# mix_out as two pairs of column blocks, three of its eight block pairs by Strassen's seven products

## The chip, the core and the metric

The kernel runs on one core of a Trainium2 chip. Times are device microseconds of one execution. Three runs of the kernel before took 1453.27 to 1454.04 us, median 1453.58 us. A separate execution was profiled; the rows below are from it.

TensorE (PE) multiplies; its weight loads (PEld) overlap its matmuls. VectorE (DVE) and ScalarE (ACT) compute elementwise, GpSimd (POOL) does little here. SyncE (SP) and ScalarE issue the DMAs.

## The reference

One decoder layer on 256 tokens of width 2048, in float32: two gated mixers side by side, then cross-attention, MLP and the final norm. The part around the change is:

```python
merged = jax.nn.sigmoid(ga) * y_attn + jax.nn.sigmoid(gc) * y_conv
x = x + merged @ w_mix_out                      # (256, 2048) @ (2048, 2048)
hq = heads(rms_norm(x, norm_xattn) @ wq_x, N_XATTN_HEADS)
mk, mv = jnp.split(rms_norm(mem, norm_mem) @ wkv_x, 2, axis=-1)
...
u = jax.nn.relu(rms_norm(x, norm_mlp) @ w_up)
return x + (u * u) @ w_down
```

## The kernel before

Each float32 operand is split into a rounded high part and the rest (`whi` and `wlo` of a weight, two planes of an activation), and a product is three matmuls: high by high, high by low, low by high (`tok_steps`, lines 108 to 110). ScalarE rounds (`split_w`, line 71), VectorE subtracts (line 72). Weights are read once from DRAM, in loads of 512 KB into four `raw` buffers; `whi` and `wlo` have five buffers each of 128 x 1024.

A product with tokens as rows is made in one of two ways.

- `tok_group` takes one block of 512 columns. It walks the 2048-deep axis in 16 steps of 128, for both halves of the tokens (h), with two PSUM banks: 16 x 2 x 3 = 96 matmuls of 512 columns.
- `pair_group` takes two neighbouring column blocks at once. It walks the axis in eight *block pairs* (two 128-deep steps each). A pair and the two token halves and the two column blocks form a 2 x 2 by 2 x 2 block product. A *plain pair* makes it in eight products (24 matmuls). A *seven-pair* makes it by Strassen's method in Winograd's form, in seven (21 matmuls). It needs sums of weight blocks (`weight_sums`, lines 139 to 142), which are then split like weights, one split of a single block (`split_one`, line 132), and sums of the activation blocks (`act_sums`), which are made once. At the end four block sums (lines 209 to 212) recombine the banks. It uses eight PSUM banks: six `acc` and both `aps`.

PSUM has six `acc` banks and two `aps`; the transposes by which `to_features` turns tokens into features (line 262) also use `aps`. Scratch blocks of 128 x 1024 (`blk`) have three buffers.

Before the change three of the four column pairs of the gate products (line 475) and all of w_down run by `pair_group`, in the order of pairs `MIXED`: seven-pairs 0 to 2 alternate with plain pairs 3 to 5, then 6 and 7. mix_out runs by `residual`: four times `tok_group`, after each an add of the residual rows `xtok` (2 MB, loaded when the gates' buffer `tok` is free), a sum of squares, eight transposes, and four scaled splits into `x2g`. After each of the four stands one call of `memory(j)`: two loads on ScalarE's queue (a quarter of the memory tokens by features, and by tokens), four scaled splits into `memT`, two sums of squares. The memory's key product, from `memT`, follows mix_out.

The order of instructions on each engine is made by the scheduler of the tile layer when the program is built; no table in the kernel sets it. Each engine runs its own list in order and waits on semaphores.

The lines that a sentence can't say, of `pair_group`:

```python
for q, a, b in ((1, act(0, 0), b11), (2, act(1, 0), b21), (3, s4, b22), (5, s1, t1), (7, s3, t3),
                (6, s2, t2), (4, act(1, 1), t4)):
    add(q, pair, a, b, True, True)
...
for q, h, j in ((2, 0, 0), (3, 0, 1), (4, 1, 0), (8, 1, 1)):
```

## Time and profile before

| | |
|---|---|
| median of three runs | 1453.58 us |
| profiled execution | 1452.71 us |
| its span, first to last instruction | 1450.9 us |
| PE busy | 1433.7 us |
| DVE busy | 1025.6 us |
| ACT busy | 752.2 us |
| mix_out stage on PE | about 549 to 640 us |

The span is what the profile shows of the execution; 1.8 us lie around it. A busy share is a share of the span. A matmul's duration in the profile overlaps with the next one's, so PE's pace is read from the distance of two starts, and what an engine waited for from the brackets at the end of a row.

### The profile page before, as it was taken

To read this page: it belongs to the slowest core of one execution; us is meant where nothing else is said; L and a number is where in the kernel's file an instruction comes from. 1 tells how busy PE (TensorE), PEld (TensorE's weight loads), DVE (VectorE), ACT (ScalarE), POOL (GpSimd) and SP (SyncE) were. 2 spreads that over 40 slices of the span, in tenths; PEclk is the share of its full clock that TensorE was granted. 3 is DMA by queue.
4 is the path that set the end of the run, shared out by engine and by line. 5 is a ranking of instruction groups with operands and counts; after the bars stand their busy time and mean duration, and the time that the engine had idled before them with its cause. 6 is when DMAs were issued, how large, how long until landed. Compare 5 with 4: busy or idle time off the path is not lost.

```text
span 1450.9 us, 18458 instructions
## 1 busy us (share of the span) xinstructions
PE 1433.7 (99%) x6923; PEld 1200.4 (83%) x6923; DVE 1025.6 (71%) x1346; ACT 752.2 (52%) x999; POOL 14.4 (1%) x20
## 2 busy tenths in 40 slices
PE   8999999999999999999999999999999999999997
PEld 6888888888878888888888888888888888888875
DVE  6645555667679756654477689668896689866897
ACT  7644444445445545564565455445554555444553
POOL 0000000000000000000000000000000000000010
PEclk9999999999999999999999999999999999999999
DMA  9766555565656767755556566665665556655554
GB/s 320 231 192 185 169 176 172 170 193 189 198 169 196 233 221 266 237 186 186 162 174 183 181 194 211 192 196 170 199 217 190 188 161 212 219 192 183 179 176 145
DMA packets 122938, 283.39 MB, mean 195 GB/s; under 512 B 8928, under 2 KB 9696, under 8 KB 122464
## 3 DMA queue, kind: packets, MB, share of 16 engines
q1 hardware_dynamic: 119088, 273.58, 59.7%
q10 hardware_dynamic: 3760, 8.63, 1.8%
q8 instruction: 54, 0.88, 0.3%
q14 instruction: 36, 0.29, 0.1%
HBM read 280.08 MB, written 2.10 MB: 194 GB/s over the span
## 4 chain that ended last, share of the span: by engine, by line
PE 95%; DVE 2%; DMA 1%; ACT 0%; issue 0%; POOL 0%; SPq 0%; POOLq 0%; DVEq 0%; ACTq 0%
PE acc L83 15%; PE acc L108 13%; PE acc L110 13%; PE acc L109 13%; PE acc L84 8%; PE acc L172 6%; PE acc L173 6%; PE acc L171 6%; PE aps L171 4%; PE aps L172 4%; PE aps L173 4%; DMA raw<-in_w_in_dram 1%; PE acc L87 1%; PE aps L262 1%; DVE wlo L72 1%; PE acc L86 1%
## 5 line engine op out<-in xcount | busy, mean ns | idle before, releaser
L72 DVE TENSOR_TENSOR wlo<-raw,whi 128x1024 fp32r<-128x1024 f32 (+1 forms) x483 | 581.0, 1213 | 307.6 <-ACT whi L71 301.9
L71 ACT ACTIVATE whi<-raw 128x1024 fp32r<-128x1024 f32 (+1 forms) x483 | 500.5, 1050 | 401.2 <-PE acc L110 134.2
L83 PE MATMUL acc<-S,whi 128*128 128x512 f32 x960 | 341.6, 398 | 0.0
L108 PE MATMUL acc<-whi,S 128*128 128x512 f32 x816 | 315.5, 389 | 5.0 <-ACT whi L71 5.0
L110 PE MATMUL acc<-whi,S 128*128 128x512 f32 x816 | 317.3, 389 | 0.0
L109 PE MATMUL acc<-wlo,S 128*128 128x512 f32 x816 | 316.7, 388 | 0.0
L84 PE MATMUL acc<-S,wlo 128*128 128x256 f32 x960 | 269.6, 281 | 0.0
L83 PEld LDWEIGHTS acc<-S,whi 128*128 128x128 f32 x960 | 180.2, 188 | 41.1
L84 PEld LDWEIGHTS acc<-S,wlo 128*128 128x128 f32 x960 | 181.3, 189 | 3.1
L108 PEld LDWEIGHTS acc<-whi,S 128*128 128x128 f32 x816 | 153.6, 189 | 35.4 <-ACT whi L71 5.7
L109 PEld LDWEIGHTS acc<-wlo,S 128*128 128x128 f32 x816 | 153.7, 188 | 30.4
L110 PEld LDWEIGHTS acc<-whi,S 128*128 128x128 f32 x816 | 153.6, 188 | 30.2
L71 ACT ACTIVATE whi<-tsum 128x1024 fp32r<-128x1024 f32 x66 | 69.3, 1058 | 92.0 <-DVE tsum L142 41.8
L172 PE MATMUL acc<-wlo,S 128*128 128x512 f32 x255 | 99.6, 391 | 0.0
L173 PE MATMUL acc<-whi,S 128*128 128x512 f32 x255 | 99.1, 389 | 0.0
L172 PE MATMUL aps<-wlo,S 128*128 128x512 f32 (+1 forms) x253 | 98.3, 388 | 0.0
L173 PE MATMUL aps<-whi,S 128*128 128x512 f32 (+1 forms) x253 | 98.1, 388 | 0.0
L171 PE MATMUL aps<-whi,S 128*128 128x512 f32 (+1 forms) x253 | 95.4, 389 | 0.7 <-DVE tok L610 0.7
L171 PE MATMUL acc<-whi,S 128*128 128x512 f32 x255 | 92.5, 389 | 0.0
L72 DVE TENSOR_TENSOR wlo<-tsum,whi 128x1024 fp32r<-128x1024 f32 x66 | 79.1, 1219 | 15.1 <-ACT whi L71 14.2
L172 PEld LDWEIGHTS acc<-wlo,S 128*128 128x128 f32 x255 | 47.9, 188 | 10.9 <-DVE wlo L72 1.0
L171 PEld LDWEIGHTS aps<-whi,S 128*128 128x128 f32 x253 | 47.5, 188 | 11.3 <-DVE tok L610 1.1
(171 smaller groups left out, 1352.2 us busy)
## 6 DMA issues: line engine op xcount, KB each, us to landing
raw<-in_w_in_dram SPq DMA_DIRECT2D x156, 512.0 KB, 4.4
raw<-in_w_up_dram SPq DMA_DIRECT2D x128, 512.0 KB, 3.9
raw<-in_w_down_dram SPq DMA_DIRECT2D x128, 512.0 KB, 4.7
raw<-in_w_mix_out_dram SPq DMA_DIRECT2D x32, 512.0 KB, 5.0
raw<-in_w_attn_out_dram SPq DMA_DIRECT2D x16, 512.0 KB, 4.9
raw<-in_w_conv_out_dram SPq DMA_DIRECT2D x16, 512.0 KB, 4.5
raw<-in_wkv_x_dram SPq DMA_DIRECT2D x16, 512.0 KB, 4.4
raw<-in_wq_x_dram SPq DMA_DIRECT2D x8, 512.0 KB, 4.0
```

Source lines behind the costliest of these rows:

```text
L71: last_split[0] = nc.scalar.activation(hi[:, k:k + step, :], raw[:, k:k + step, :], AF.Copy)
L72: nc.vector.tensor_sub(lo[:, k:k + step, :], raw[:, k:k + step, :], hi[:, k:k + step, :].bitcast(F32))
L83: nc.tensor.matmul(ps, a, xs(k, 2), start=(k == 0), stop=False)
L84: nc.tensor.matmul(ps[:, S:], c, xs(k, 0), start=False, stop=False)
L86: nc.tensor.matmul(ps[:, S:], c, xs(k, 0), start=False, stop=False)
L87: nc.tensor.matmul(ps, a, xs(k, 2), start=(k == 0), stop=True)
L108: nc.tensor.matmul(ps, xh, wh, start=(k == 0), stop=False)
L109: nc.tensor.matmul(ps, xh, wl, start=False, stop=False)
L110: nc.tensor.matmul(ps, xl, wh, start=False, stop=(k == nk - 1))
L171: nc.tensor.matmul(ps, ah, bh, start=first, stop=False)
L172: nc.tensor.matmul(ps, ah, bl, start=False, stop=False)
L173: nc.tensor.matmul(ps, al, bh, start=False, stop=final)
```

## The change

mix_out is no longer four `tok_group`s but two `pair_group`s (group 1 is columns 0 to 1023, group 2 the rest), with a new order `HIGH`: block pairs 5, 6 and 7 by seven products, and 0 to 4 plain. Pairs 5 to 7 are the features 1280 to 2047 of the merged gates. Their activation sums are made into a new buffer `mS`, where the merged features come out of the transposes (`ev_m`): there a copy to a `blk` goes first, then `act_sums`, then the split. The residual add takes two operations per block in place of one. The transposes of a group follow it, eight features blocks in a row in place of four, and two calls of `memory` stand after each group.

```diff
--- before.py
+++ after.py
@@ -153,7 +153,7 @@
         nc.vector.tensor_sub(s4, a12, s2)
         split_act(dst, kk, t)
 
-    def pair_group(w, c0, kr0, nk, xs, xsum, order, evac, fine=False):
+    def pair_group(w, c0, kr0, nk, xs, xsum, order, evac, fine=False, base=0):
 
         bank = {}
         last = {}
@@ -189,7 +189,7 @@
                 b21, b22 = split_w(r[1])
                 t1, t3 = split_w(ta)
                 t2, t4 = split_w(tb)
-                s1, s2, s3, s4 = (tuple(xsum[:, pair, p, i * P:(i + 1) * P] for p in range(2)) for i in range(4))
+                s1, s2, s3, s4 = (tuple(xsum[:, pair - base, p, i * P:(i + 1) * P] for p in range(2)) for i in range(4))
                 for q, a, b in ((1, act(0, 0), b11), (2, act(1, 0), b21), (3, s4, b22), (5, s1, t1), (7, s3, t3),
                                 (6, s2, t2), (4, act(1, 1), t4)):
                     add(q, pair, a, b, True, True)
@@ -222,6 +222,7 @@
             evac(h, j, bank[8][:, lo], u[:, lo], lo)
             evac(h, j, bank[9][:, lo], u[:, hi], hi)
 
+    HIGH = [(5, True), (0, False), (6, True), (1, False), (7, True), (2, False), (3, False), (4, False)]
     WHOLE, HALVES = (slice(0, 512),), (slice(0, 256), slice(256, 512))
     MIXED = [(0, True), (3, False), (1, True), (4, False), (2, True), (5, False), (6, False), (7, False)]
     MIXED2 = [(0, True), (3, False), (1, True), (4, False), (2, True), (5, False), (6, False), (7, False)]
@@ -473,6 +474,8 @@
                     tok_group(w_in, c0 + j * 512, 0, KD, hx, ev_s)
             else:
                 pair_group(w_in, c0, 0, KD, hx, hS, MIXED, ev_g)
+        if jp:
+            mS = big.tile([P, 3, 2, 512], F32R, name="SS")
         for c in range(2):
             o = c * 512
 
@@ -487,12 +490,38 @@
             tok_group(w_conv_out, jp * 1024 + o, 0, 8, parts_of(acT, 8), ev_v)
 
             def ev_m(b, pt, jp=jp, c=c):
-                split_act(mg, 8 * jp + 4 * c + b, pt.rearrange("p (k s) -> p k s", k=2), 2)
+                k = 8 * jp + 4 * c + b
+                z = pt.rearrange("p (k s) -> p k s", k=2)
+                if k >= 10:
+                    z = block()[:, 0, :].rearrange("p (k s) -> p k s", k=2)
+                    nc.scalar.activation(z, pt.rearrange("p (k s) -> p k s", k=2), AF.Copy)
+                    act_sums(mS, k // 2 - 5, z)
+                split_act(mg, k, z, 2)
             to_features(sg[:, 0, :, o:o + 512], 0, 4, ev_m)
 
     xtok = big.tile([P, 2, D], F32, name="tok")
     nc.sync.dma_start(xtok, xv)
 
+
+    def residual_pairs(w, xs, xsum, dst, gi, name, between):
+        sp = const.tile([P, 2, 4], F32, name=name + "sp")
+        for jp in range(2):
+            def ev(h, j, ps, u, jp=jp):
+                c = 2 * jp + j
+                t = xtok[:, h, c * 512:(c + 1) * 512]
+                nc.vector.tensor_add(t, u, t)
+                nc.vector.tensor_add(t, ps, t)
+                sumsq(sp[:, h, c:c + 1], t, 512)
+
+            def ev_f(b, pt, jp=jp):
+                for i in range(2):
+                    k = 8 * jp + b + i
+                    split_scaled(dst, k, pt[:, i * S:(i + 1) * S], g_of(gi, k))
+            pair_group(w, jp * 1024, 0, KD, xs, xsum, HIGH, ev, base=5)
+            to_features(xtok, 8 * jp, 8, ev_f)
+            between(2 * jp)
+            between(2 * jp + 1)
+        return sp
 
     def residual(w, nk, xs, dst, gi, name, between=lambda j: None):
         sp = const.tile([P, 2, 4], F32, name=name + "sp")
@@ -524,7 +553,7 @@
         for h in range(2):
             sumsq(rmsp[:, h, j:j + 1], mt[:, h, :], 512)
 
-    sp2 = residual(w_mix_out, KD, parts_of(mg), x2g, 1, "r2", memory)
+    sp2 = residual_pairs(w_mix_out, parts_of(mg), mS, x2g, 1, "r2", memory)
     rm = rstd(rmsp, "rm")
     r2 = rstd(sp2, "r2")
 
```

How the scheduler's order moves, at three places.

VectorE, between two column blocks of mix_out before: splits of weights (L72), residual adds (L502), scaled splits of transposed features into `S1` (`x2g`) and of memory into `S3` (`memT`).

```order
L72 TENSOR_TENSOR wlo_4594<-raw_4591,whi_4593 128x1024
L72 TENSOR_TENSOR wlo_4600<-raw_4597,whi_4599 128x1024
L502 TENSOR_TENSOR tok_4397<-acc_4403,tok_4397 128x512
L72 TENSOR_TENSOR wlo_4630<-raw_4627,whi_4629 128x1024
L502 TENSOR_TENSOR tok_4397<-acc_4404,tok_4397 128x512
L72 TENSOR_TENSOR wlo_4636<-raw_4633,whi_4635 128x1024
L72 TENSOR_TENSOR wlo_4666<-raw_4663,whi_4665 128x1024
L72 TENSOR_TENSOR wlo_4672<-raw_4669,whi_4671 128x1024
L252 SCALAR_TENSOR_TENSOR S1_4399<-aps_4555,gcol_88,S1_4399 128x256
L252 SCALAR_TENSOR_TENSOR S1_4399<-aps_4564,gcol_88,S1_4399 128x256
L72 TENSOR_TENSOR wlo_4702<-raw_4699,whi_4701 128x1024
L252 SCALAR_TENSOR_TENSOR S3_4400<-blk_5131,gcol_88,S3_4400 128x256 x4
```

VectorE at the boundary of group 1 and group 2 after the change: `blk_4820` and `blk_4836` are the memory blocks of `memory(0)` and `memory(1)`, L513 the adds that empty group 1's banks, `tsum` the weight sums of group 2's seven-pairs.

```order
L253 SCALAR_TENSOR_TENSOR S3_4428<-blk_4820,gcol_88,S3_4428 128x256 x4
L142 TENSOR_TENSOR tsum_4857<-raw_4854,tsum_4857 128x512
L72 TENSOR_TENSOR wlo_4871<-tsum_4856,whi_4870 128x1024
L253 SCALAR_TENSOR_TENSOR S3_4428<-blk_4836,gcol_88,S3_4428 128x256 x4
L513 TENSOR_TENSOR tok_4425<-acc_4461,tok_4425 128x512
L513 TENSOR_TENSOR tok_4425<-acc_4465,tok_4425 128x512
L139 TENSOR_TENSOR tsum_4947<-raw_4943 128x512
L72 TENSOR_TENSOR wlo_4875<-tsum_4857,whi_4874 128x1024
L513 TENSOR_TENSOR tok_4425<-aps_4481,tok_4425 128x512
L513 TENSOR_TENSOR tok_4425<-aps_4515,tok_4425 128x512
L72 TENSOR_TENSOR wlo_4911<-raw_4906,whi_4910 128x1024
L72 TENSOR_TENSOR wlo_4915<-raw_4908,whi_4914 128x1024
```

Two memory blocks' splits now stand ahead of the adds that empty the banks, and weight sums and splits of the next group between them.

ScalarE at the memory loads in mix_out before (`S_4400` is `memT`):

```order
L523 DMA blk<-in_mem_dram 128x2x512
L71 ACTIVATE whi<-raw 128x1024
L519 DMA blk<-in_memf_dram 128x1024
L247 ACTIVATE S_2391<-aps 128x2x256 x2
L251 ACTIVATE S_4400<-blk,gcol 128x256 x4
L71 ACTIVATE whi<-raw 128x1024 x2
L523 DMA blk<-in_mem_dram 128x2x512
L71 ACTIVATE whi<-raw 128x1024 x2
```

ScalarE at the same place after the change (`S_4428` is `memT`, `tsum` a weight sum of group 2):

```order
L548 DMA blk<-in_memf_dram 128x1024
L71 ACTIVATE whi<-raw 128x1024 x2
L252 ACTIVATE S_4428<-blk,gcol 128x256 x4
L552 DMA blk<-in_mem_dram 128x2x512
L548 DMA blk<-in_memf_dram 128x1024
L71 ACTIVATE whi<-tsum 128x1024
L252 ACTIVATE S_4428<-blk,gcol 128x256 x4
L552 DMA blk<-in_mem_dram 128x2x512
L71 ACTIVATE whi<-tsum 128x1024
L71 ACTIVATE whi<-raw 128x1024 x2
```

In the piece of before one load and one block's scaling belong to this boundary; after the change two do, and the first block's scaling stands ahead of the issue of the second block's load.

PE at a boundary of column blocks before: transposes of finished columns stand among the matmuls of the next, which use other banks (`acc`).

```order
L109 MATMUL acc_4589<-wlo_4600,S2_2391 128x512
L262 MATMUL aps_4555<-ident_108,tok_4397 128x128
L262 MATMUL aps_4564<-ident_108,tok_4397 128x128
L110 MATMUL acc_4589<-whi_4599,S2_2391 128x512
...
L110 MATMUL acc_4590<-whi_4599,S2_2391 128x512
L262 MATMUL aps_4555<-ident_108,tok_4397 128x128 x3
L262 MATMUL aps_4564<-ident_108,tok_4397 128x128 x3
L108 MATMUL acc_4590<-whi_4599,S2_2391 128x512
```

PE in group 2 after the change: the last transposes of group 1 (`aps_4802`, `aps_4811`), and, eleven matmuls further, the first matmul of group 2 on an `aps` bank (`aps_4902`).

```order
L171 MATMUL acc_4878<-ohi_5036,S2_2391 128x512
L263 MATMUL aps_4802<-ident_108,tok_4425 128x128 x4
L263 MATMUL aps_4811<-ident_108,tok_4425 128x128 x4
L171 MATMUL acc_4898<-whi_4965,SS_4061 128x512
...
L173 MATMUL acc_4882<-whi_4994,S2_2391 128x512
L172 MATMUL acc_4886<-wlo_4995,S2_2391 128x512
L173 MATMUL acc_4886<-whi_4994,S2_2391 128x512
L171 MATMUL aps_4902<-whi_4874,S2_2391 128x512
L172 MATMUL aps_4902<-wlo_4875,S2_2391 128x512
```

The products on `aps` banks, which stood in program order among the others, now come after the transposes have left these banks.

## Rows read from the trace of the kernel before

**Rows 1.** The page: busy time by engine; the granted clock in 40 slices.

```profile
PE 1433.7 (99%) x6923; PEld 1200.4 (83%) x6923; DVE 1025.6 (71%) x1346; ACT 752.2 (52%) x999; POOL 14.4 (1%) x20
...
PEclk9999999999999999999999999999999999999999
```

**Rows 2.** Waits of PE: line, whom for, us in total, times, longest.

```profile
PE acc L108 <- ACT whi L71: 5.0, 2, 4.6
PE aps L171 <- DVE tok L610: 0.7, 1, 0.7
PE acc L171 <- ACT ohi L131: 0.5, 1, 0.5
PE acc L171 <- ACT whi L71: 0.4, 1, 0.4
PE acc L108 <- ACT SS L247: 0.3, 1, 0.3
PE acc L172 <- DVE olo L132: 0.2, 1, 0.2
```

**Rows 3.** Timeline of PE in mix_out: start, us, engine, line, tiles, count.

```profile
540.06 0.39 PE L110 MATMUL acc<-whi,S 128*128 128x512 f32 x1
...
551.85 0.39 PE L108 MATMUL acc<-whi,S 128*128 128x512 f32 x1
...
557.56 0.82 PE L262 MATMUL aps<-ident,tok 128*128 128x128 f32 x6
558.13 0.48 PE L108 MATMUL acc<-whi,S 128*128 128x512 f32 x1
```

**Rows 4.** Windows (mix_out; two w_down groups): length, busy PE PEld DVE ACT POOL, clock.

```profile
549.00:640.00 91.00, 91.00 (x419) 75.32 (x418) 56.66 (x72) 53.66 (x89) 0.00 (x0) 1.00 0.72 238
1019.00:1060.00 41.00, 41.00 (x181) 33.71 (x180) 38.31 (x46) 20.77 (x23) 0.00 (x0) 1.00 0.58 181
1060.00:1102.00 42.00, 42.00 (x200) 35.12 (x200) 33.34 (x37) 19.07 (x21) 0.00 (x0) 1.00 0.71 232
```

**Rows 5.** Timeline of DVE, in w_down and in mix_out.

```profile
1035.11 1.21 DVE L72 TENSOR_TENSOR wlo<-raw,whi 128x1024 fp32r<-128x1024 f32 x1
1036.25 0.68 DVE L210 TENSOR_TENSOR blk<-acc,blk 128x512 f32<-128x512 f32 x1
1036.85 0.68 DVE L211 TENSOR_TENSOR blk<-acc,blk 128x512 f32<-128x512 f32 x1
...
587.48 4.63 DVE L72 TENSOR_TENSOR wlo<-raw,whi 128x1024 fp32r<-128x1024 f32 x4 [0.40 <-ACT whi L71]
...
552.94 2.85 DVE L252 SCALAR_TENSOR_TENSOR S<-blk,gcol,S 128x256 fp32r<-128x256 f32 x7
```

**Rows 6.** Timeline of ACT in mix_out, with its DMA issues (ACTq).

```profile
555.04 1.06 ACT L71 ACTIVATE whi<-raw 128x1024 fp32r<-128x1024 f32 x1 [0.32 <-PE acc L110]
...
561.75 1.71 ACT L251 ACTIVATE S<-blk,gcol 128x256 fp32r<-128x256 f32 x4 [2.58 <-DMA blk<-in_memf_dram]
563.36 1.05 ACT L71 ACTIVATE whi<-raw 128x1024 fp32r<-128x1024 f32 x1
564.01 0.37 ACTq L523 DMA_DIRECT2D blk<-in_mem_dram  x1
```

**Rows 7.** The memory loads by features: issue min/median/max ns, and landing.

```profile
L519 ACTq DMA_DIRECT2D blk<-in_memf_dram x4: 347/347/347, 501.7 to 578.3; - x4
...
DMA to landing us min/median/max: 5.1/5.8/5.9
```

**Rows 8.** Groups of DVE, shapes apart: count, busy us, mean ns, idle before.

```profile
L72 DVE TENSOR_TENSOR wlo<-raw,whi 128x1024 fp32r<-128x1024 f32 x475 | 575.6, 1222 | 306.8 <-ACT whi L71 301.2
L209 DVE TENSOR_TENSOR blk<-acc,blk 128x512 f32<-128x512 f32 x11 | 7.5, 682 | 0.0
L252 DVE SCALAR_TENSOR_TENSOR S<-blk,gcol,S 128x256 fp32r<-128x256 f32 x16 | 6.7, 479 | 3.9 <-ACT S L251 3.9
```

**Rows 9.** mix_out's loads: landing; issues from 555 to 575 us; SP, ACT.

```profile
DMA to landing us min/median/max: 3.8/5.0/13.4
...
raw<-in_w_mix_out_dram SPq DMA_DIRECT2D x6, 512.0 KB, 8.0
tok<-in_x_dram SPq DMA_DIRECT2D x1, 2048.0 KB, 11.6
...
558.41 0.37 SPq L494 DMA_DIRECT2D tok<-in_x_dram  x1
558.87 40.11 SPq L61 DMA_DIRECT2D raw<-in_w_mix_out_dram  x15
...
572.39 1.06 ACT L71 ACTIVATE whi<-raw 128x1024 fp32r<-128x1024 f32 x1 [6.08 <-DMA raw<-in_w_mix_out_dram]
```

**Rows 10.** Timelines of DVE and PE in the second gate group.

```profile
430.20 0.69 DVE L139 TENSOR_TENSOR tsum<-raw 128x512 f32<-128x512 f32 x1 [3.19 <-DMA raw<-in_w_in_dram]
...
430.89 0.49 PE L171 MATMUL acc<-ohi,S 128*128 128x512 f32 x1 [0.47 <-ACT ohi L131]
```

## The prediction

> **What bounds the kernel now.** I read the page first: TensorE (PE) is busy for 99% of the span at the full granted clock, VectorE (DVE) for 71% [rows 1]. Then the waits of PE: the few rows there are add up to some 7 us, 5.0 of them at the start of the kernel [rows 2]. So the kernel lasts as long as PE's instruction stream. A matmul taken away is worth its own step, and everything else is free until PE waits for it. Third, PE's steps in the mix_out stage: 52 matmuls of 512 columns start between 540.06 and 551.85 us, 0.2267 us each, and six transposes take 558.13 - 557.56 = 0.57 us, 0.095 us each [rows 3]. Last, the load beside PE. In the whole mix_out stage (549 to 640 us) DVE is busy 56.7 of 91 us; where `pair_group` already runs twice in a row, in w_down, it is busy 38.3 of 41 us and then 33.3 of 42 us, and PE still does not wait [rows 4]. So a pair group nearly fills DVE, and mix_out has other DVE work that w_down has not.
>
> **What it removes.** Three of eight block pairs take 21 matmuls in place of 24, in two column pairs: 2 x 3 x 3 = 18 matmuls, 18 x 0.2267 = 4.1 us off PE [rows 3]. The transposes stay at 32, the weight bytes at 32 loads of 512 KB. By the instruction orders nothing moves ahead of the first mix_out weights or behind the attention that follows, so no other stage has a term.
>
> **What it adds, on DVE.** Durations overlap by a little, so I count from start to start: a 512-wide operation 0.60 us (1036.25 to 1036.85), a 1024-wide split 1.14 us (1035.11 to 1036.25, and four in 4.63 us), a 256-wide scaled split 0.40 us (seven in 2.85 us) [rows 5]. A plain pair costs two splits, 2.28 us. A seven-pair costs four sums, one 512-wide split and three 1024-wide ones: 4 x 0.60 + 0.60 + 3 x 1.14 = 6.42 us, 4.14 us more. Six of them: 24.8 us. Four block sums per group: 2 x 4 x 0.60 = 4.8 us. Sixteen residual adds in place of eight: 4.8 us. The activation sums of `mS` are three times four 128-wide operations and a split; I take 1.4 us each from the 0.60 us of the split and an estimate of 0.2 us for a 128-wide one, together 4.3 us. The sum is 38.7 us. With the 56.7 us of before DVE has 95 us of work in a stage in which PE has 91 - 4.1 = 87 us. Buffers can lend a few us of that, so the place at which DVE is furthest behind decides.
>
> **That place is the boundary of the two groups.** In the last third of group 1 DVE is tied to PE: the split of pair 3 (`wlo_4693`) needs one of five `whi` buffers, and the first to come free is that of pair 7, when PE has done its last matmul on `whi_4619`. I set that moment to 0. ScalarE's split follows, 1.06 us [rows 6], with hand-overs 1.2 us by my estimate. From there DVE's order holds, up to the second scaled split of `aps_4802`: 13 splits of 1024 (14.8 us), 26 operations of 512 (15.6 us) and 15 scaled splits of 256 (6.0 us), 36.4 us in all. PE has in the same piece, up to the first matmul on `aps_4902`, 137 matmuls and 16 transposes: 31.1 + 1.5 = 32.6 us. That matmul needs the PSUM bank that held `aps_4802`. So it comes (1.2 + 36.4) - 32.6 = 5.0 us late even if DVE waits for nothing.
>
> **DVE waits there too.** Both `memory` calls now stand at one place. Their blocks come free when the sums `x`, `y` and `z` of group 1 have been used. The last reader of `x` ends at 1.2 + 2 x 1.14 + 3 x 0.60 = 5.3 us. A memory load lands 5.8 us after its issue [rows 7]: 11.1 us. ScalarE then scales four pieces, 1.71 us as at 561.75 us, and only behind them does it issue a DMA, as at 564.01 us [rows 6]. So the second `memory` load is issued at about 13.3 us (0.4 us of it for the load of `mt` between them) and lands at 19.1 us; the first piece is ready at 19.6 us. DVE stands at its first split for that load at 5.3 + 4 x 1.14 + 9 x 0.60 + 4 x 0.40 = 16.9 us and waits 2.7 us. Behind this instruction are queued the four adds that free group 1's banks, the splits of group 2's first two pairs and all eight scaled splits of the transposes; PE waits for each of them in turn. The delay goes through: 5.0 + 2.7 = 7.7 us. From the other sides: with landings of 5.1 and 5.9 us in both loads [rows 7] the wait is 1.3 to 2.9 us; without any, the stall stays at 5.0 us.
>
> Two rules would move this term. The four memory loads of before landed after 5.1 to 5.9 us [rows 7]. The Trainium skill (SBUF — State Buffer, "The DMA setup-cost knee") puts a transfer at about 2 us and its bytes at 436 GB/s. An estimate by that page is 3.2 us for 512 KB; two loads in a row would then be 5.2 us sooner, the wait gone, and the total 2.7 us less. The trace does not agree, so I keep its landings. A DVE operation of 0.68 us is followed by the next after 0.60 us [rows 5]. The Trainium skill (VectorE: DVE Perf Modes, "The DRAIN you can't avoid") says that the next operation does not start before the pipe of the one before is empty. If that meant durations end to end, 1.222, 0.682 and 0.479 us [rows 8], the 36.4 us would be 40.8 and the total 4.4 us more. The starts go against it.
>
> **A smaller term in group 1.** The third seven-pair's second row load is issued just before the 2 MB residual load. DVE has 4.4 us of other work before it needs that row, and PE a margin of 1.9 us beyond; the landing thus costs PE what it exceeds 6.3 us by. Landings in this stage are 3.8 us at the least, 5.0 in the median and 13.4 us at the most, with 8.0 in the median beside the residual load [rows 9]: 0 to 7.1 us, 1.7 at 8.0 us. I take 0.7 us. That such a late row stops PE is seen in the gates: DVE waited 3.19 us for one at 430.20 us, and PE 0.47 us at 430.89 us for what hangs on it [rows 10]. ScalarE gets no term of its own: six more 1024-wide splits at 1.06 us [rows 6] and, at about half of that each, 14 more 512-wide splits and copies are some 14 us on top of 53.7 of 91 us [rows 4]. After the boundary DVE is again tied to PE by buffers, and the next stage's weights need only half as many splits per matmul, so nothing is lost there; the lost time is not regained either, since PE was full.
>
> **Sum.** The profiled execution took 1452.71 us, span 1450.9 and 1.8 us around it. -4.1 + 7.7 + 0.7 = +4.3 us, so 1457.0 us. The median of the runs, 1453.58 us, lies 0.9 us above the profiled execution, so 1457.9 us is what I expect of the runs. Of the term of 7.7 us, a 3% error in the steps moves 1.1 us and the memory landings 1.4 us; with 0 to 1.7 us for group 1 the forecast's own range is 1455 to 1461 us.
>
> **Rivals.**
> 1. *The buffers hold as in the other pair groups.* DVE gets ahead in the plain pairs, the boundary is only rough, and PE waits no more than in all the pair groups of before together, the 1.8 us of the four L171 and L172 rows [rows 2]. For it: DVE at 38.3 of 41 us in w_down did no harm [rows 4], and PE waits for pair groups so little in the whole trace. Against it: the five buffers are what ties DVE, and between the two w_down groups stand no transposes and no memory loads. -4.1 + 0.6 = -3.5 us, 1450.1 us: faster. It decides if fewer than about 1.2 us of DVE's 7.7 us lag reach PE. Chance 0.11.
> 2. *DVE is behind, but not through memory.* The second memory load lands before DVE gets there and part of the 5.0 us is made good by steps that are shorter beside PSUM reads. A stall of 4 to 5 us: -4.1 + 4.5 = +0.4 us, 1454.0 us, no change. For it: a 5.1 us landing already halves the wait. Chance 0.20.
> 3. *The residual load decides.* The row load beside it lands after 13.4 us as one did before [rows 9], PE waits 7.1 us in group 1, of which the tie to PE's buffers afterwards spares nothing: +4.3 + 6.4 = +10.7 us, 1464 us. Against it: that landing was of the load issued at 558.87 us, behind the residual load (ScalarE got it at 572.39 us); this one is issued ahead. Chance 0.12.
> The forecast itself has 0.57.
>
> **Chances and range.** A measurement tells 0.2%, 2.9 us, from no change. Faster by more: nearly all of rival 1 with its small stalls, 0.10. Within: rival 2, and the low end of the forecast, 0.23. Slower: the rest of the forecast and rival 3, 0.67. The range 1451.5 to 1463.5 us leaves out most of rival 1 and half of rival 3, and takes in everything else.
>
> **What would show it.** Right: PE's matmul records in the mix_out stage fall by 18; the waits of PE have new rows that name L171 to L173 and the transposes, waiting for VectorE, within some 25 us around the end of group 1, and sum to 6 to 11 us; the largest single one is the first matmul on an `aps` bank in group 2; DVE is busy all but 3 us there, and has one wait for the memory load of some 2.7 us through ScalarE. Wrong: PE with no gap at the boundary (then the five buffers did not tie DVE, rival 1); a gap there with DVE idle for other reasons, as row loads (rival 3); or new waits outside 545 to 645 us, since the order elsewhere is unchanged.

## The result and the profile after

The changed kernel takes 1466.89 us (median of four runs, 1464.44 to 1468.69) against 1453.42 us for the kernel before beside it: a ratio of 1.0085, 95% interval 1.0068 to 1.0102. It is slower, as predicted, but by 13.5 us where 4.3 were predicted, and above the upper end of the range, 1463.5 us. The profiled execution took 1468.69 us, its span 1466.9 us.

The page of the changed kernel: busy time by engine, and the granted clock in 40 slices.

```profile
PE 1439.1 (98%) x6905; PEld 1201.9 (82%) x6905; DVE 1062.7 (72%) x1413; ACT 764.2 (52%) x1019; POOL 15.5 (1%) x20
...
PEclk9999999999999999899999999999999999999999
```

Against [rows 1], 18 matmul records are gone, as they should be, and yet PE's busy time has *grown* by 5.4 us. That contradiction is the first clue, and the clock line holds the second: one slice shows 8 where all of before showed 9.

The waits of PE after (line, whom for, us in total, times, longest):

```profile
PE acc L108 <- ACT whi L71: 4.8, 1, 4.8
PE acc L171 <- ACT whi L71: 4.2, 2, 3.9
PE acc L171 <- ACT ohi L131: 2.1, 2, 1.5
PE aps L171 <- DVE S L253: 1.9, 1, 1.9
PE acc L171 <- DVE tok L639: 1.3, 2, 0.9
PE aps L263 <- DVE tok L513: 1.3, 1, 1.3
```

The first row is the kernel's start, in [rows 2] as well. To place the rest I lay the two profiles side by side at two points of PE: the last transposes ahead of mix_out and the first matmul of w_up. Before, then after:

```profile
534.38 0.82 PE L262 MATMUL aps<-ident,tok 128*128 128x128 f32 x6
...
740.82 0.39 PE L83 MATMUL acc<-S,whi 128*128 128x512 f32 x1
```

```profile
537.91 0.82 PE L263 MATMUL aps<-ident,tok 128*128 128x128 f32 x6
...
755.35 0.39 PE L83 MATMUL acc<-S,whi 128*128 128x512 f32 x1
```

This stretch, which I call the stage below, took 206.44 us before and 217.44 us after: 11.0 us more. 3.5 us were lost ahead of it and 1.5 us behind it. Inside it, the timeline of PE with every row after 540 us and ahead of 700 us that waited, and some of their neighbours:

```profile
560.98 0.50 PE L171 MATMUL aps<-whi,S 128*128 128x512 f32 x1 [0.36 <-ACT blk L497]
...
598.53 0.39 PE L173 MATMUL acc<-whi,SS 128*128 128x512 f32 x1
602.81 1.22 PE L171 MATMUL acc<-whi,S 128*128 128x512 f32 x2 [3.90 <-ACT whi L71]
603.83 0.63 PE L171 MATMUL acc<-whi,SS 128*128 128x512 f32 x1
604.26 0.63 PE L172 MATMUL acc<-wlo,SS 128*128 128x512 f32 x1
...
608.30 0.48 PE L172 MATMUL acc<-wlo,S 128*128 128x512 f32 x1
...
613.46 0.50 PE L172 MATMUL acc<-wlo,SS 128*128 128x512 f32 x1 [0.31 <-DVE wlo L72]
...
615.24 0.50 PE L171 MATMUL acc<-ohi,S 128*128 128x512 f32 x1 [0.58 <-ACT ohi L131]
...
618.59 0.51 PE L172 MATMUL acc<-wlo,S 128*128 128x512 f32 x1 [0.26 <-DVE wlo L72]
...
619.40 0.40 PE L173 MATMUL acc<-whi,S 128*128 128x512 f32 x1
621.67 0.59 PE L171 MATMUL aps<-whi,S 128*128 128x512 f32 x1 [1.87 <-DVE S L253]
622.06 0.63 PE L172 MATMUL aps<-wlo,S 128*128 128x512 f32 x1
...
625.39 0.39 PE L171 MATMUL aps<-whi,S 128*128 128x512 f32 x1
...
658.80 1.25 PE L263 MATMUL aps<-ident,tok 128*128 128x128 f32 x8 [1.27 <-DVE tok L513]
```

Read the starts as well as the brackets. From 603.83 to 604.26 us one matmul takes 0.43 us; its step is 0.2267 us in [rows 3]. Steps as long stand behind the wait at 621.67 us. The windows of PE show why (length, busy PE PEld DVE ACT POOL, granted clock):

```profile
599.00:603.00 4.00, 0.19 (x1) 0.19 (x2) 3.30 (x7) 3.84 (x7) 0.00 (x0) 0.80 0.52 162
603.00:607.00 4.00, 4.00 (x10) 3.02 (x11) 4.00 (x6) 4.00 (x10) 0.00 (x0) 0.50 0.01 3
617.00:622.00 5.00, 2.87 (x11) 1.66 (x10) 5.00 (x10) 2.25 (x6) 0.00 (x0) 0.99 0.44 120
622.00:626.00 4.00, 4.00 (x12) 3.15 (x11) 1.74 (x2) 1.06 (x1) 0.00 (x0) 0.59 0.31 115
```

After PE stood still, its granted clock was 0.50, the lower of its two levels (1.2 against 2.4 GHz), for some 4 us. A PE at half clock counts as busy, so the page's busy time grows while work was taken away.

Now the stage's account. The gaps, from start to start less one step, are 4.05 us at 602.81, 0.48, 0.75, 0.43 and, at 621.67, 2.04 us: 7.75 us at the boundary. Nine matmuls and eight transposes from 602.81 to 608.30 us took 5.49 us; at the steps of [rows 3] they take 9 x 0.2267 + 8 x 0.095 = 2.80 us. Nine matmuls from 621.67 to 625.39 us took 3.72 us in place of 2.04. So 2.7 + 1.7 = 4.4 us went to the half clock. The wait at 560.98 us cost 0.6 us, that at 658.80 us 1.4 us. -4.1 + 7.75 + 4.4 + 0.6 + 1.4 = 10.1 us; 0.9 of the 11.0 us is spread over smaller shifts that I did not place. This says how PE spent the time, not what each term would give back if it alone were gone.

Who holds PE at 602.81 us is seen on ScalarE (ACTq is its DMA issue):

```profile
585.72 0.35 ACTq L548 DMA_DIRECT2D blk<-in_memf_dram  x1
...
592.65 0.51 ACT L252 ACTIVATE S<-blk,gcol 128x256 fp32r<-128x256 f32 x1 [4.16 <-DMA blk<-in_memf_dram]
...
593.08 0.48 ACTq L548 DMA_DIRECT2D blk<-in_memf_dram  x1
...
599.16 0.51 ACT L252 ACTIVATE S<-blk,gcol 128x256 fp32r<-128x256 f32 x1 [3.85 <-DMA blk<-in_memf_dram]
...
600.77 1.04 ACT L71 ACTIVATE whi<-tsum 128x1024 fp32r<-128x1024 f32 x1
601.72 1.99 ACT L71 ACTIVATE whi<-raw 128x1024 fp32r<-128x1024 f32 x2
```

The second `memory` load is issued only when the first has landed, at 593.08 us, beside the second of the four scalings and not behind all four as predicted. ScalarE then stands for it, and the weight splits for PE's next matmuls are queued behind. VectorE waits beside it, 1.24 us for the first load's scaling and 3.08 us for the second's:

```profile
599.70 1.68 DVE L253 SCALAR_TENSOR_TENSOR S<-blk,gcol,S 128x256 fp32r<-128x256 f32 x4 [3.08 <-ACT S L252]
...
621.04 0.87 DVE L253 SCALAR_TENSOR_TENSOR S<-aps,gcol,S 128x256 fp32r<-128x256 f32 x2
```

The first of the two splits at 621.04 us takes 0.48 us and frees the `aps` bank, and PE starts on it at 621.67 us. Between these two rows VectorE stands for only 0.85 us (0.67 and 0.18 us for `whi`). So this matmul could hardly have come sooner, however soon PE had done what stands ahead of it: the 3.90 us wait for `whi` and the 2.7 us of slow steps behind it lie inside a time that VectorE needed anyway. Two paths hold PE here at once, ScalarE's line and VectorE's.

The loads by features now land after (minimum, median, maximum)

```profile
DMA to landing us min/median/max: 6.0/6.5/9.2
```

where [rows 7] had 5.1, 5.8 and 5.9. The two of the boundary took 6.9 and 6.1 us, the last one, behind group 2, 9.2 us, and VectorE stood for it:

```profile
655.28 0.49 DVE L253 SCALAR_TENSOR_TENSOR S<-blk,gcol,S 128x256 fp32r<-128x256 f32 x1 [5.11 <-ACT S L252]
```

The Trainium skill (SBUF — State Buffer, "The DMA setup-cost knee") would give an estimate of 3.2 us for their 512 KB; the trace does not agree, with 6.0 us at the least.

### The profile page after: what moved, and what is told of

Same layout as the page of the kernel before. It is cut to its first block, busy times and chain, and to the rows that moved or that the text cites. A ratio compares the mean times of both kernels' runs of the same rounds, so it can differ in the third digit from the quotient of the medians.

```text
span 1466.9 us, 18527 instructions
## 1 busy us (share of the span) xinstructions
PE 1439.1 (98%) x6905; PEld 1201.9 (82%) x6905; DVE 1062.7 (72%) x1413; ACT 764.2 (52%) x1019; POOL 15.5 (1%) x20
## 4 chain that ended last, share of the span: by engine, by line
PE 83%; DMA 7%; DVE 7%; ACT 1%; issue 1%; POOL 0%; POOLq 0%; ACTq 0%; DVEq 0%; SPq 0%
PE acc L83 15%; PE acc L108 10%; PE acc L109 10%; PE acc L110 10%; PE acc L84 7%; PE acc L172 5%; PE acc L171 5%; PE acc L173 5%; PE aps L171 4%; PE aps L172 3%; PE aps L173 3%; DMA raw<-in_w_down_dram 3%; DVE wlo L72 3%; DMA blk<-in_memf_dram 2%; DMA raw<-in_w_mix_out_dram 2%
## 5 line engine op out<-in xcount | busy, mean ns | idle before, releaser
L72 DVE TENSOR_TENSOR wlo<-raw,whi 128x1024 fp32r<-128x1024 f32 (+1 forms) x477 | 573.5, 1213 | 275.6 <-ACT whi L71 270.9
L108 PE MATMUL acc<-whi,S 128*128 128x512 f32 (+1 forms) x688 | 265.8, 390 | 4.8 <-ACT whi L71 4.8
L110 PE MATMUL acc<-whi,S 128*128 128x512 f32 (+1 forms) x688 | 267.4, 389 | 0.0
L109 PE MATMUL acc<-wlo,S 128*128 128x512 f32 (+1 forms) x688 | 267.3, 388 | 0.0
L108 PEld LDWEIGHTS acc<-whi,S 128*128 128x128 f32 x688 | 129.9, 189 | 30.8 <-ACT whi L71 5.4
L110 PEld LDWEIGHTS acc<-whi,S 128*128 128x128 f32 x688 | 129.9, 189 | 25.4
L109 PEld LDWEIGHTS acc<-wlo,S 128*128 128x128 f32 x688 | 129.9, 189 | 25.3
L71 ACT ACTIVATE whi<-tsum 128x1024 fp32r<-128x1024 f32 x78 | 81.8, 1058 | 97.4 <-DVE tsum L142 42.3
L172 PE MATMUL acc<-wlo,S 128*128 128x512 f32 (+1 forms) x301 | 117.7, 392 | 0.3 <-DVE wlo L72 0.3
L172 PE MATMUL aps<-wlo,S 128*128 128x512 f32 x299 | 117.5, 393 | 0.0
L171 PE MATMUL aps<-whi,S 128*128 128x512 f32 x299 | 114.5, 394 | 2.9 <-DVE S L253 1.9
L173 PE MATMUL aps<-whi,S 128*128 128x512 f32 x299 | 117.1, 392 | 0.0
L173 PE MATMUL acc<-whi,S 128*128 128x512 f32 (+1 forms) x301 | 116.9, 389 | 0.0
L171 PE MATMUL acc<-whi,S 128*128 128x512 f32 (+1 forms) x301 | 109.5, 392 | 3.9 <-ACT whi L71 3.9
L72 DVE TENSOR_TENSOR wlo<-tsum,whi 128x1024 fp32r<-128x1024 f32 x78 | 93.8, 1223 | 12.3 <-ACT whi L71 11.3
L171 PEld LDWEIGHTS acc<-whi,S 128*128 128x128 f32 x301 | 56.5, 189 | 16.7 <-ACT whi L71 4.6
L171 PEld LDWEIGHTS aps<-whi,S 128*128 128x128 f32 x299 | 56.9, 190 | 16.2 <-issue 2.3
```

The source lines that it names most:

```text
L71: last_split[0] = nc.scalar.activation(hi[:, k:k + step, :], raw[:, k:k + step, :], AF.Copy)
L72: nc.vector.tensor_sub(lo[:, k:k + step, :], raw[:, k:k + step, :], hi[:, k:k + step, :].bitcast(F32))
L108: nc.tensor.matmul(ps, xh, wh, start=(k == 0), stop=False)
L109: nc.tensor.matmul(ps, xh, wl, start=False, stop=False)
L110: nc.tensor.matmul(ps, xl, wh, start=False, stop=(k == nk - 1))
L171: nc.tensor.matmul(ps, ah, bh, start=first, stop=False)
```

## The experiments

Two theories stood first. **A:** ScalarE's queue, held by the second memory load, stops PE, and the halved clock adds to it. **B:** VectorE simply has more work at the boundary than PE's time covers. **C** came after the first four runs: whatever stands on ScalarE and VectorE ahead of the scaled splits that free the two `aps` banks reaches PE, since products 4 and 8 of the next group need these banks. Each ratio is to the kernel before in the same comparison. The stage is from one profile each.

| run | ratio to before, 95% interval | stage, us |
|---|---|---|
| changed kernel | 1.0085 [1.0068, 1.0102] | 217.4 |
| 1 memory constant | 1.0064 [1.0046, 1.0083] | 214.8 |
| 2 loads first | 1.0039 [1.0025, 1.0053] | 212.5 |
| 3 sums late | 1.0031 [1.0014, 1.0048] | 212.8 |
| 4 plain pairs only | 1.0062 [1.0045, 1.0078] | 216.8 |
| 5 transposes later | 1.0053 [1.0034, 1.0073] | 213.8 |
| 6 = 2 and 5 | 1.0024 [1.0012, 1.0035] | 210.0 |
| 7 = 2, 3 and 5 | 0.9995 [0.9983, 1.0007] | 206.5 |
| 8 = 4 with filling | 1.0057 [1.0035, 1.0079] | 215.0 |
| 9 = 2 and 3 | 1.0033 [1.0018, 1.0048] | 210.3 |
| 10 = 7, transposes spread | 0.9976 [0.9967, 0.9985] | 203.7 |
| changed kernel again | 1.0075 [1.0061, 1.0089] | 216.4 |

**1. Memory constant.** The loads by features are left out and a constant tile is scaled in their place, behind the copy of bank 1 in each group, so `memT` holds other values. (In all the edits below `...` marks lines that are not shown; where an edit repeats that of an earlier run, only some of its lines stand here.)

```diff
-        m = block().rearrange("p a (b s) -> p (a b) s", s=S)
-        nc.scalar.dma_start(m, memf[:, 4 * j:4 * j + 4, :])
-        for k in range(4):
-            split_scaled(memT, 4 * j + k, m[:, k, :], g_of(2, 4 * j + k))
+        with tc.issue_after(last_p1[0].ins):
+            for k in range(4):
+                split_scaled(memT, 4 * j + k, ones, g_of(2, 4 * j + k))
```

> Left out: the four loads of the memory tokens by features; the scalings that read them read a constant tile instead, and stand behind the copy of bank 1 in each group. Theory A (ScalarE's queue stands still for the second memory load, PE waits 3.9 us for a weight split behind it, and pays again by the halved clock): the 3.9 us wait of PE at the end of group 1 is gone, ScalarE has no idle time of 4 us there, and the total falls by 5 to 8 us, to 1459 to 1462 us. Theory B (VectorE has too much work at the boundary, whoever waits first): ScalarE's idle time goes, PE's waits stay within 2 us of the changed kernel's, total 1464 to 1468 us.

It took 1464.0 us. The 3.9 us wait for ScalarE is gone, but another came, in the waits of PE:

```profile
PE aps L173 <- DVE S L255: 5.0, 1, 5.0
```

The total is B's, the place is the one that the prediction named, and 5.0 us is what it gave for "DVE waits for nothing". But that agreement is luck, and the run does not decide for B. With no load to wait for, the scheduler put the eight scalings of *group 2's* memory blocks into this stretch, 3.2 us of VectorE's work at the 0.40 us of a step, right ahead of the splits that free the bank:

```profile
612.29 2.46 DVE L255 SCALAR_TENSOR_TENSOR S<-ones,gcol,S 128x256 fp32r<-128x256 f32 x6
```

The eight of group 1, in turn, left the boundary for 574 us. What VectorE does here without a wait for the loads and without these is seen in run 2.

**2. Loads first.** Four `blk` buffers; both loads are issued ahead of both scalings.

```diff
-    blk = ctx.enter_context(tc.tile_pool(name="blk", bufs=3))
+    blk = ctx.enter_context(tc.tile_pool(name="blk", bufs=4))
...
+        for i in range(2):
+            m = block().rearrange("p a (b s) -> p (a b) s", s=S)
+            nc.scalar.dma_start(m, memf[:, 4 * (j + i):4 * (j + i) + 4, :])
+            ms.append(m)
```

> Four scratch blocks in place of three, and both memory loads of a boundary issued ahead of the first scaling; the work is the same. Theory A: one landing is waited for in place of two, the wait of PE for the split behind it shrinks from 3.9 to under 1.5 us, total 4 to 7 us less than the changed kernel, 1460 to 1463 us. Theory B: no more than 2 us less, 1465 to 1468 us.

1460.02 us, the stage 4.9 us shorter: A's outcome, but waits of 0.2 to 1.9 us are left at the boundary (`wlo` 1.01, `ohi` 1.56, an `aps` bank 1.89 us), so not A alone. VectorE does not stand for a memory load at the boundary any more. Even so the gaps of PE up to the first matmul on an `aps` bank (1.17, 0.89, 1.73, 0.41 and 2.05 us, start to start less a step) add up to 6.3 us, where the prediction gave 5.0 us for "DVE waits for nothing". That part of B is shown.

**3. Sums late.** Group 2 begins with two plain pairs.

```diff
+    LATE = [(0, False), (1, False), (5, True), (2, False), (6, True), (3, False), (7, True), (4, False)]
...
-            pair_group(w, jp * 1024, 0, KD, xs, xsum, HIGH, ev, base=5)
+            pair_group(w, jp * 1024, 0, KD, xs, xsum, LATE if jp else HIGH, ev, base=5)
```

> Group 2 takes plain pairs 0 and 1 before its seven-pairs, so that the weight sums of pair 5 leave the boundary (4.1 us less VectorE work there); the memory loads stay. Theory A: the wait of PE for ScalarE behind the memory load stays at 3 to 5 us, total within 2 us of the changed kernel. Theory B: the waits of PE in group 2 fall by about 4 us and with them one stretch of half clock (2 us), total 1460 to 1463 us.

1459.4 us, the stage 4.7 us shorter, a little more than B expected and with the memory loads untouched. The largest wait of PE at the boundary is 1.06 us, where A had expected 3 to 5 us, although VectorE stands 4.90 us for the second load here.

**4. Plain pairs only.** Two groups of eight plain pairs: no weight or activation sums at all, and the 18 matmuls are back.

```diff
-    HIGH = [(5, True), (0, False), (6, True), (1, False), (7, True), (2, False), (3, False), (4, False)]
+    HIGH = [(k, False) for k in range(8)]
```

> Both groups by pair_group with plain pairs alone: no weight sums, activation sums or block sums, 384 matmuls as before; boundary, transposes and memory loads stay where the change puts them. Theory A: the wait behind the memory load stays and costs 3 to 4 us and a stretch of half clock, total 1457 to 1461 us. Theory B: without the sums VectorE keeps up, PE waits under 1 us, total 1453 to 1455 us.

1463.27 us, above what either theory expected. PE has one large wait, and for eight matmuls behind it half the clock:

```profile
612.54 0.77 PE L171 MATMUL aps<-whi,S 128*128 128x512 f32 x1 [6.54 <-DVE S L257]
```

ScalarE shows its origin:

```profile
608.76 1.71 ACT L256 ACTIVATE S<-blk,gcol 128x256 fp32r<-128x256 f32 x4 [4.50 <-DMA blk<-in_memf_dram]
```

VectorE waits 4.52 us beside it, and the scaled splits that free the banks are queued behind on both engines. So the pairing by itself, eight banks in use and two `memory` calls in one place, costs a stall without any of Strassen's sums. This run made theory C.

**5. Transposes later.** All 32 of them follow the memory key product.

```diff
-            to_features(xtok, 8 * jp, 8, ev_f)
+            feats.append(lambda jp=jp, ev_f=ev_f: to_features(xtok, 8 * jp, 8, ev_f))
...
     by_features(wkv_x, xm, rm, mkT)
+    for feat in feats:
+        feat()
```

> All 32 feature transposes of the mixed rows (with their scaled splits) stand behind the memory key product, so that the two aps banks belong to products 4 and 8 alone at the boundary of the column groups; memory's loads and scalings stay where they are. Theory A (ScalarE's queue held by the second memory load): the wait for whi remains with 3 to 4 us, followed by steps of 0.43 us, and only the aps waits go: 1462 to 1466 us. Theory B (VectorE has too much at the boundary): the scaled splits of the transposes are gone from it, so 1456 to 1460 us and no wait above 1.3 us. Theory C (what stands on ScalarE and VectorE ahead of the hand-over of the two aps banks reaches TensorE): the aps waits of 1.9 and 1.3 us and the slow steps behind the first go, the whi wait shrinks only as far as the queue is shorter: 1458 to 1462 us.

1461.3 us. Both `aps` waits are gone; the wait for `whi` stays at 3.67 us, and half-clock steps follow it until 604.5 us. C and A are both seen in one trace: the banks were one way to PE, ScalarE's line the other.

**6. Transposes later and loads first**, the edits of 2 and 5.

```diff
+    blk = ctx.enter_context(tc.tile_pool(name="blk", bufs=4))
...
+            feats.append(lambda jp=jp, ev_f=ev_f: to_features(xtok, 8 * jp, 8, ev_f))
```

> As the run with the transposes behind the memory key product, and both memory loads are issued ahead of the scalings, with four blk buffers in place of three. Theory C with A: neither the banks nor the loads hold anything at the boundary, no wait above 1 us in mix_out, no half-speed steps there, so the 18 matmuls saved show: 1449 to 1453 us, up to 1455 if the gates stall as in the changed kernel. Theory B: waits for wlo and ohi stay (VectorE's sums): 1456 to 1460 us.

1458.89 us. At the boundary only waits of 0.2 to 0.8 us are left and no half clock, but the stage is still 3.6 us longer than before. Higher than C and A expected: waits for `ohi` and `wlo` stay at the boundary, as B said, and behind it come new ones, 0.56, 0.56 and 1.35 us between 660 and 719 us.

**7. All three**, the edits of 2, 3 and 5.

```diff
+            pair_group(w, jp * 1024, 0, KD, xs, xsum, LATE if jp else HIGH, ev, base=5)
...
+            feats.append(lambda jp=jp, ev_f=ev_f: to_features(xtok, 8 * jp, 8, ev_f))
```

> As the run before it, and the second column group begins with two plain block pairs, so that its first sums come some 10 us after the boundary. Theory C with A: nothing left for it to mend, within 1.5 us of the run without it. Theory B: 3 us faster than the run without it or more.

1454.15 us; the stage is 3.6 us shorter than without the late sums, which is B's expectation. With two of the three alone, loads and transposes (run 6) or loads and sums (run 9), the kernel stays slower than before. Whether the loads are needed beside the other two is not shown: the third pair was not run. The stage now equals that of before, 206.45 against 206.44 us. Of the 4.1 us saved, 2.8 us are spent again on four small waits, 0.36, 0.56, 0.56 and 1.35 us, the last three behind the boundary, between 656 and 714 us.

**8. Plain pairs with filling.** As 4, with 28 useless matmuls more (the first of a product, repeated and overwritten) ahead of the place of the 6.54 us.

```diff
+            for _ in range(28 if base and c0 and q == 3 and first else 0):
+                nc.tensor.matmul(ps, ah, bh, start=True, stop=True)
             nc.tensor.matmul(ps, ah, bh, start=first, stop=False)
```

> The kernel of plain pairs alone (384 matmuls), with 28 useless matmuls more (a product's first one, repeated and overwritten) in the second column group, ahead of the place where TensorE stood 6.54 us. If the half granted clock follows the pause, TensorE's granted clock stays at 1.00 through the stretch, no step of 0.43 us stands there, and the time is that of the kernel without them or 1 to 2 us below it (1461 to 1463.5), though 6.3 us of work were added. If the low clock has nothing to do with the pause, the slow steps stay and the time is 0 to 2 us above; if the pause is not a wait with an end of its own, the time grows by 6 us, to 1469.

1462.46 us, though 28 x 0.2267 = 6.3 us of work were added; the ratios, 1.0057 and 1.0062, do not tell the two kernels apart. The stage is 1.8 us *shorter*, in one profile each. Windows of run 4, then of this run:

```profile
604.00:612.00 8.00, 2.01 (x13) 1.51 (x12) 3.33 (x9) 3.27 (x9) 0.00 (x0) 0.82 0.41 159
612.00:616.00 4.00, 3.46 (x8) 2.82 (x9) 0.79 (x2) 0.28 (x1) 0.00 (x0) 0.50 0.00 0
```

```profile
604.00:612.00 8.00, 8.00 (x41) 6.68 (x40) 3.52 (x8) 3.53 (x8) 0.00 (x0) 1.00 0.08 31
612.00:616.00 4.00, 4.00 (x19) 3.31 (x18) 1.42 (x2) 2.51 (x3) 0.00 (x0) 1.00 0.00 0
```

ScalarE still waits 3.77 us for the memory load, so the origin is unchanged; PE only did not stand. With the pause the low clock is gone: nine steps on the `aps` bank took 2.07 us here and 3.77 us in run 4. The half clock follows the pause, and here it is a price of its own. The Trainium skill (TensorE: Matmul & The Clock Gate, "HAM oscillation — how this bites in real kernels") tells of a kernel whose PE waits for a transfer ahead of each piece of work and starts each piece throttled. Run 4 agrees, with a clock of 0.50 behind 6.54 us; that the short wait of 1.87 us in the changed kernel did it too goes beyond the page's case.

**9. Loads first and sums late**, the edits of 2 and 3, transposes left at the boundary.

```diff
+            pair_group(w, jp * 1024, 0, KD, xs, xsum, LATE if jp else HIGH, ev, base=5)
             to_features(xtok, 8 * jp, 8, ev_f)
```

> Loads first and sums late together, but the transposes stay at the boundary of the column groups. Theory C (the aps banks as well): an aps wait of 1 us or more stays at the boundary, 2 to 4 us above the run with all three (ratio to the kernel before 1.001 to 1.003). Rival (loads and sums alone): within 1 us of the run with all three (ratio 0.999 to 1.0005).

1460.09 us: C's size, but not C's mechanism. No `aps` wait of 1 us is there; the largest wait is

```profile
608.48 0.80 PE L171 MATMUL acc<-ohi,S 128*128 128x512 f32 x1 [3.14 <-ACT ohi L131]
```

and ScalarE got that row's data at 607.80 us. The row's load was issued only at 602.4 us and landed 5.3 us later; its issue had waited for VectorE, whose weight sums read the `raw` buffer before. So VectorE's line is at the origin here too, by way of a buffer and not of a bank. Another 2.7 us were lost in the gates, outside the stage, with a wait of 1.72 us and half clock behind it. That the transposes must leave the boundary is shown (runs 7 and 9); that it is always by the banks is not.

**10. Transposes spread.** As 7, but the transposes stand ahead of the memory key product in the program, and the scheduler spreads them through it.

```diff
+    for feat in feats:
+        feat()
     by_features(wkv_x, xm, rm, mkT)
-    for feat in feats:
-        feat()
```

> The run with everything mended (loads first, sums late, transposes behind group 2), but the transposes stand ahead of the memory key product in the program, so that the scheduler spreads them through its 22 us. The waits of 0.56, 0.56 and 1.35 us of that run between 656 and 712 us should go. Theory C (what was saved is lost at each hand-over of the two aps banks): 2 to 3 us below that run, so 2 to 4 us below the kernel before in the same comparison (ratio 0.997 to 0.999). Rival: the transposes meet group 2's last hand-overs and a wait of the same size stands there: no gain against the kernel before (ratio 0.999 to 1.001).

1450.7 us against 1453.94 us: **0.9976 [0.9967, 0.9985], faster than both kernels.** The three waits behind the boundary are gone, and PE does not pause in it:

```profile
590.00:630.00 40.00, 40.00 (x178) 32.94 (x177) 35.29 (x43) 27.86 (x42) 0.00 (x0) 1.00 0.67 226
```

VectorE is fuller there than in the changed kernel, 35.29 against 31.05 us in the same window, in which PE was busy for 33.08 us at a mean clock of 0.87. So the amount of VectorE's work over these 40 us does not by itself stop PE; its order does, and the waits for loads in it. The stage is 2.8 us shorter than before.

**The changed kernel again**, with no edit, for a second profile.

> The changed kernel once more, for a second profile of the gates, whose order the change leaves alone. If the stall of 1.5 us for ohi there and the half clock behind it are of one execution, the start of mix_out moves by 1 to 3 us between the two profiles and the waits in mix_out (3.9 for whi, 1.9 for an aps bank) return at the same instructions within 1 us. If the change shifts the gates, the stall returns there too. The ratio to the kernel before is 1.006 to 1.010 in both cases.

1464.89 us. In the gates of the first profile PE had waited 1.53 us for `ohi`, with half clock behind; the second shows 0.17 us, before had 0.47 us [rows 10]. Windows of the gates, the first profile and then the second:

```profile
434.00:438.00 4.00, 4.00 (x12) 3.04 (x11) 4.00 (x6) 3.15 (x4) 0.00 (x0) 0.57 0.43 130
```

```profile
434.00:438.00 4.00, 4.00 (x19) 3.31 (x18) 4.00 (x6) 3.40 (x5) 0.00 (x0) 1.00 0.61 164
```

So the stall in the gates varies from one execution of the changed kernel to the next. Waits of 1.16 to 1.72 us for this `ohi` stand in the profiles of runs 2, 3, 6 and 9 too; the kernel before has one profile only, so how often it stalls there is not shown. mix_out's loss returned, 9.9 us of stage: 5.28 us for the same `whi`, 0.88 us for the `aps` bank. Each moved by 1.0 to 1.4 us, a little more than expected. The second memory load landed after 8.4 us this time, and VectorE stood 4.99 us for it. The wait of 1.27 us for the last transposes did not return; the last load landed after 6.8 us here and after 9.2 us in the first profile.

## Why the prediction was wrong, and where it was right

- **PE is the bound, -4.1 us:** right. 18 matmul records fewer; run 10 brings back 2.8 us of them.
- **7.7 us at the boundary:** the path was right, the size was not. The term is how late the first matmul on an `aps` bank comes. Counted so it is 10.4 us: the five gaps and the 2.7 us of slow steps ahead of it. That the gaps alone add up to 7.75 us is luck. VectorE's work came out as forecast: 36.4 us less the 15.7 us ahead of the second load's splits leave 20.7 us, and the trace has 21.0 us without the waits. The step that failed is the wait put at 2.7 us: VectorE stood 1.24 + 3.08 us for the two memory loads, which landed after 6.9 and 6.1 us in place of 5.8, and 0.85 us for `whi` from ScalarE, 5.2 us in all.
- **"ScalarE gets no term of its own":** this failed beside it. It was argued from the sum of ScalarE's work, 54 of 91 us, where the order of its line decides: an engine half idle can still hold PE if one instruction in its line waits for a load. The longest wait of PE was for `whi`, from ScalarE, and not for the `aps` bank as the prediction's signs had it. In the changed kernel this wait ran beside VectorE's delay; run 5 shows it by itself, 3.67 us with no `aps` wait left at the boundary.
- **What was missing: the clock.** The prediction priced a pause at its length. Half-clock steps can follow it, 4.4 us in the stage, and run 8 shows that they go with the pause. The 1.7 us behind the `aps` wait come on top of the term; that the 2.7 us ahead of it cost time of their own is not shown. The profile of before held a sign of this: behind PE's waits at the kernel's start, 5.0 us in [rows 2], steps are 0.43 us, although the granted clock from 7 to 8 us reads 1.00 there.

```profile
7.23 0.63 PE L109 MATMUL acc<-wlo,S 128*128 128x512 f32 x1
7.66 0.63 PE L110 MATMUL acc<-whi,S 128*128 128x512 f32 x1
```

- **"After the boundary nothing is lost":** wrong by 1.4 us in the first profile; in the second no such wait stands there. The last memory load of the first landed after 9.2 us, VectorE stood 5.11 us for its scaling, and the adds that empty group 2's banks were queued behind, so the last transposes came late.
- **Group 1, 0.7 us for a late row:** that wait did not come; 0.6 us was lost for another reason, ScalarE's copy of merged features at L497, which an `aps` bank waits for (560.98 us).
- **Waits only within 545 to 645 us:** the wait at 658.80 us stands outside. In the first profile 3.5 us were lost ahead of the stage, 2.6 of them in the gates, and 1.5 us behind it; the second profile has no such stall in the gates.
- **Rivals:** the first (buffers hold) fell with the 7.75 us of gaps, where it allowed 1.2. The second (not through memory) fell with the 3.08 and 4.99 us that VectorE stood for the second load. The third gave 1464 us, near the time, but no row load stopped PE in group 1.

For the first profile: 2.7 us more at the boundary, 1.7 us of half clock behind it, 1.4 us behind the boundary and 0.9 us unplaced turn the predicted +4.3 into +11.0 us of stage. The medians stand 13.5 and, in the second comparison, 10.95 us apart; what lies between these two is not explained.

## What to carry to other kernels

A stall of TensorE can cost half-speed steps behind it on top of its length: look at the clock of the window after each pause. Before adding up the waits in a trace, ask which of them would still be there if the one ahead were gone; two paths may hold one engine at the same place. Before two jobs are merged at one place, write down each engine's line there in order and ask what waits for a load in it: a load's consumer in a shared line stops everything behind it, however idle that engine is on average. If an arithmetic saving lands slower, move what stands at the boundary (issue loads together, start the next group with the cheap pieces, spread the transposes) before giving the saving up; here only run 10, which has all of these, came out faster than before.

## What the runs showed that I had not expected

A pause's length alone did not tell whether the half clock follows. The same matmul, the first on an `aps` bank in group 2, waited 1.87 us in the changed kernel, and the steps behind it were 0.42 us. In run 2 it waited 1.89 us, and they stayed at 0.23 us:

```profile
619.93 0.47 PE L171 MATMUL aps<-whi,S 128*128 128x512 f32 x1 [1.89 <-DVE S L253]
620.24 0.39 PE L172 MATMUL aps<-wlo,S 128*128 128x512 f32 x1
620.47 0.39 PE L173 MATMUL aps<-whi,S 128*128 128x512 f32 x1
```

It was the same in the gates: PE waited 1.55 us for `ohi` in run 6 and the steps behind stayed at 0.23 us, while 1.22 us in run 2 were followed by steps of 0.42 us.

And useless work can cost nothing: 6.3 us of it, laid into a 6.5 us pause, left the time where it was and the stage 1.8 us shorter.
